# One hybrid decoder layer on one core: the last head's output rows, its decays and k's transposition in another order, and a wider pin in the first feed-forward stage

## The chip, the cores and the metric

The kernel runs on one core of one Trainium2 chip. The metric is the time of one execution on the device in microseconds; lower is better. All arithmetic that counts is done by TensorE (PE) in pairs of a high and a low part, three products for one product of float32, so that PE is busy nearly all the time, and VectorE (DVE) and ScalarE (ACT) make the high and low parts, copy results out of PSUM and compute the nonlinear steps. GpSimd (POOL) does little, and SyncE (SP) issues nearly all transfers.

## The reference, cut to what matters

```python
x = x + 0.5 * swiglu(rms_norm(x, n1), w_gate1, w_up1, w_down1)     # FFN 1: silu(h Wg) * (h Wu), then Wd
h = rms_norm(x, mix_norm)                                          # 1024 tokens, width 1024
proj = h @ w_in                      # q, k, v, z of 8 heads of 128; z, x, B, C of 16 SSM heads; gates
qkv = silu(causal_dwconv(proj_qkv, conv_w))                        # 4 taps
q, k = l2_normalize(q) * 128**-0.5, l2_normalize(k)
decay = exp(where(incl, gc[t] - gc[s], -inf))                      # gc: running sum of log decays in a chunk of 64
a_low = where(strict, beta * (k k^T) * decay, 0); t_inv = inverse(eye + a_low)
u, w = t_inv @ (v * beta), t_inv @ (k * beta * exp(gc))
o_gdn = scan over chunks(q k^T * decay, u, w, ...)                 # state 128 x 128 per head
o_gdn = rms_norm(o_gdn, w_n) * silu(z)
o_ssm = rms_norm(ssd(...) * silu(z_ssm), ...)                      # Mamba-2, in two groups of 512
x = x + concat(o_gdn, o_ssm) @ w_out                               # 2048 rows of w_out
x = x + 0.5 * swiglu(rms_norm(x, n2), w_gate2, w_up2, w_down2)     # FFN 2
out = rms_norm(x, final_norm)
```

## The kernel before

The program is written once, in the order of its stages, and a scheduler puts the instructions of each engine in a row: it takes them by the order of the program where operands are ready by its own reckoning, and by explicit pins (`tc.issue_after(e)`: what is written inside is placed behind instruction `e`). On the chip each engine then works its row off from the front.

**FFN.** Each of the two feed-forward stages forms gate and up products by seven products of half-size blocks in place of eight (`a_ops` and `b_ops` make sums of blocks on DVE, `split` makes the high part on ACT, line 241, and the low part on DVE, line 242). `gate_up_all` goes over 22 tiles of weights (`for i, (p, w) in enumerate(todo)`), gate and up in turn; PE's products are lines 334 to 336, copies out of PSUM line 343, the gate's silu line 380 or 462. In the first stage a side stream is mixed into this loop: `win_units` reads columns of `w_in` (`wraw`), forms the seven combinations of four of the heads' weights, splits them (`wunit`, ACT 241 and DVE 242) and stores them in DRAM (`wu_scr`), and each `next(side)` issues one such piece. The loop issues none for tiles under 4, and for tile 4 a first one in the first half (only loads) and two in the second half. Line 433 decides which halves of tile 4 pin these pieces behind the sums and splits (`made`) of the same half.

**Mixer.** Four units of the SSM come first, then 8 heads (`for h in range(GH)`). Heads 0 to 3 (`h < NESTED`) project q and k (`conv_silu`: product, four taps, silu), then v and z (`proj_half`), with the weights split on the spot (lines 123 to 125 on PE). Heads 4 to 7 use the stored units (`chunk`, `unit_prod`, lines 1259 to 1261 on PE). For each head `decays` (not yet a function before) loads the running sums into `dt`, exponentiates them to `qe` (line 1361) and, block by block, to `dt` (line 1364, eight small ACT instructions, behind POOL's causal mask). `k_part` transposes k on PE (line 1345, two PSUM banks called `ps_mx`) and reads each of the 8 blocks twice on ACT: `jd` (line 1349, the squared norm) and `kd` (line 1350, k scaled by a decay). Then follow the products of k with k and q (lines 1426 and 1427, again `ps_mx` banks), small inverse steps (products of 32 and 64 columns, lines 1496 to 1522, and many small DVE instructions `fx`, `ft`), and the recurrence.

**Output projection.** The output rows are summed in `xa`. `group_tile(n, b, dh, w, m)` multiplies one group of 256 rows of `w_out` (`w`, high and low part) with the normalised SSM outputs (`m`, called `mtt`): six products into one `ps_pj` bank (lines 123 to 125, operands `w` and `mtt`), and ACT copies the bank to `xa` with a scale (line 1220) for group 0. `out_start` loads rows and outputs of group 0 on POOL's queue, splits the rows (`w0`, ACT 241, DVE 242) and makes `mtt` (`ssm_split`: high on ACT, line 1200, low on DVE, line 1201); `group_prep(1)` does the same for group 1. The first 8 tiles (`FIRST_TILES = 4` blocks by two halves) are drawn into the last head, h = 7, ahead of its k products, which are pinned behind the last of those tiles (`tile_end`).

## Time and profile before

| what | value |
|---|---|
| median of 3 runs | 2318.16 us (2317.92 to 2319.36) |
| the profiled execution | 2318.03 us, span 2316.3 us |
| PE busy | 2267.1 us, 98% of the span |
| DVE, ACT, POOL busy | 76%, 51%, 2% |
| mean granted clock of PE | 0.993 |

The span reaches from the first to the last recorded instruction; 1.7 us of the profiled execution lie outside it. PE's granted clock is 1.00 nearly everywhere and 0.50 in a few stretches. A row of the timeline has the start, the duration, the engine, the line, the operation, what it writes and reads, and in brackets how long the engine had stood idle and which instruction ended the wait. The durations of PE's rows overlap; the spacing of their starts is what one costs.

### The profile page before, as it was taken

The numbers are of one execution on the slowest core, as the hardware profiler recorded it, in microseconds if no ns is written. First come the engines' busy times: TensorE is split into PE (matmuls) and PEld (weight loads), VectorE is DVE, ScalarE is ACT, GpSimd is POOL, SyncE is SP. The second block draws the span as 40 slices with busy tenths as digits, with TensorE's granted clock in tenths as the row PEclk, the third lists the DMA queues.
The fourth block names the chain that finished last, engine by engine and source line by source line (L and its number), as shares of the span: only waits on it lengthen the run. The fifth ranks groups of instructions, "written<-read, shape, count | busy, mean of one in ns | idle before, by whom it ended". The sixth has DMA issues, their size and how long they took to land.

```text
span 2316.3 us, 31987 instructions
## 1 busy us (share of the span) xinstructions
PE 2267.1 (98%) x11654; PEld 1848.9 (80%) x11654; DVE 1753.3 (76%) x3217; ACT 1179.7 (51%) x2284; POOL 50.6 (2%) x117
## 2 busy tenths in 40 slices
PE   7999999999999999999999998999999999999998
PEld 5788888888878878877877776888878888888886
DVE  8998987769777787656667778578698777766787
ACT  7444433354367985874655557432443333334344
POOL 0000000000000110000000000000000000000000
PEclk9999999999999999999999999899999999999999
DMA  3467663496653343242356556335223333329445
GB/s 111 159 210 241 228 207 115 170 334 214 210 187 125 128 128 98 69 128 65 83 165 180 168 172 216 103 98 191 91 72 119 109 106 109 104 89 357 138 154 214
DMA packets 262194, 356.96 MB, mean 154 GB/s; under 512 B 60808, under 2 KB 167404, under 8 KB 260244
## 3 DMA queue, kind: packets, MB, share of 16 engines
q1 hardware_dynamic: 261364, 352.73, 46.7%
q8 instruction: 91, 1.49, 0.3%
q0 software_dynamic: 672, 2.19, 0.2%
q14 instruction: 67, 0.55, 0.1%
HBM read 249.34 MB, written 105.52 MB: 153 GB/s over the span
## 4 chain that ended last, share of the span: by engine, by line
PE 79%; DVE 9%; ACT 7%; DMA 2%; issue 2%; POOL 0%; SPq 0%; DVEq 0%; ACTq 0%; POOLq 0%
PE ps_pj L124 6%; PE ps_pj L123 6%; PE ps_pj L125 6%; PE ps_pj L334 6%; PE ps_pj L335 6%; PE ps_pj L336 6%; PE ps_mx L334 3%; PE ps_mx L336 3%; PE ps_mx L335 3%; PE ps_pj L564 2%; PE ps_pj L565 2%; PE ps_pj L563 2%; PE ps_pj L1259 2%; PE ps_pj L1261 2%; PE ps_pj L1260 2%
## 5 line engine op out<-in xcount | busy, mean ns | idle before, releaser
L336 PE MATMUL ps_pj<-bh,al 128*128 128x512 f32 x688 | 267.9, 389 | 0.0
L335 PE MATMUL ps_pj<-bl,ah 128*128 128x512 f32 x688 | 267.8, 389 | 0.0
L334 PE MATMUL ps_pj<-bh,ah 128*128 128x512 f32 x688 | 267.5, 390 | 0.0
L125 PE MATMUL ps_pj<-hhi,wlo 128*128 128x512 f32 x576 | 229.9, 399 | 0.0
L123 PE MATMUL ps_pj<-hhi,whi 128*128 128x512 f32 x576 | 229.4, 398 | 0.4 <-ACT gsb L901 0.4
L124 PE MATMUL ps_pj<-hlo,whi 128*128 128x512 f32 x576 | 228.9, 397 | 0.0
L335 PEld LDWEIGHTS ps_pj<-bl,ah 128*128 128x128 f32 x688 | 129.2, 188 | 26.7
L336 PEld LDWEIGHTS ps_pj<-bh,al 128*128 128x128 f32 x688 | 129.2, 188 | 26.7
L334 PEld LDWEIGHTS ps_pj<-bh,ah 128*128 128x128 f32 x688 | 129.0, 188 | 26.6
L242 DVE TENSOR_TENSOR al<-as,ah 128x512 fp32r<-128x512 f32 x220 | 141.1, 685 | 7.3 <-ACT ah L241 6.8
L317 DVE TENSOR_TENSOR as<-wst 128x512 f32<-128x512 f32 x220 | 144.3, 684 | 2.5 <-DMA wst<-in_ffn_w_up_dram 2.4
L241 ACT CAST ah<-wst 128x512 fp32r<-128x512 f32 x88 | 54.5, 621 | 179.1 <-PE ps_oo L335 116.7
L241 ACT CAST hid<-hraw 128x1024 fp32r<-128x1024 f32 (+1 forms) x84 | 82.2, 980 | 123.6 <-PE ps_oo L565 45.6
L334 PE MATMUL ps_mx<-bh,ah 128*128 128x512 f32 x352 | 139.3, 398 | 5.2 <-ACT sg L380 2.1
L335 PE MATMUL ps_mx<-bl,ah 128*128 128x512 f32 x352 | 139.0, 395 | 0.4 <-DVE bl L242 0.4
L336 PE MATMUL ps_mx<-bh,al 128*128 128x512 f32 x352 | 138.2, 393 | 1.0 <-DVE al L242 1.0
L241 ACT CAST ah<-as 128x512 fp32r<-128x512 f32 x220 | 125.2, 617 | 19.6 <-DVE as L317 19.5
L123 PEld LDWEIGHTS ps_pj<-hhi,whi 128*128 128x128 f32 x576 | 108.4, 188 | 21.6 <-ACT gsb L901 0.9
L124 PEld LDWEIGHTS ps_pj<-hlo,whi 128*128 128x128 f32 x576 | 108.4, 188 | 21.4 <-issue 0.8
L125 PEld LDWEIGHTS ps_pj<-hhi,wlo 128*128 128x128 f32 x576 | 108.3, 188 | 20.9 <-issue 0.5
L242 DVE TENSOR_TENSOR hid<-hraw,hid 128x1024 fp32r<-128x1024 f32 (+1 forms) x84 | 95.0, 1131 | 26.6 <-ACT hid L241 26.3
L343 ACT COPY m<-ps_pj 128x512 f32<-128x512 f32 x88 | 51.6, 588 | 112.9 <-PE ps_pj L336 112.7
(502 smaller groups left out, 5651.6 us busy)
## 6 DMA issues: line engine op xcount, KB each, us to landing
hraw<-hid_scr SPq DMA_DIRECT2D x70, 512.0 KB, 4.3
wu_scr<-wunit SPq DMA_DIRECT2D x112, 256.0 KB, 3.2
wunits<-wu_scr SPq DMA_DIRECT2D x56, 512.0 KB, 4.7
hid_scr<-hs SPq DMA_DIRECT2D x110, 256.0 KB, 3.0
wst<-in_ffn_w_down_dram SPq DMA_DIRECT2D x50, 512.0 KB, 4.7
wst<-in_ffn_w_gate_dram SPq DMA_DIRECT2D x22, 1024.0 KB, 5.6
wst<-in_ffn_w_up_dram SPq DMA_DIRECT2D x22, 1024.0 KB, 5.5
hid_scr<-sg SPq DMA_DIRECT2D x44, 256.0 KB, 2.0
```

The lines of the kernel that those rows point to most:

```text
L123: T.matmul(o, lhsT=wh, rhs=mh, start=first, stop=False)
L124: T.matmul(o, lhsT=wh, rhs=ml, start=False, stop=False)
L125: return T.matmul(o, lhsT=wl, rhs=mh, start=False, stop=last)
L241: return (A.copy(out=hi, in_=src), V.tensor_tensor(out=lo, in0=src, in1=hi.bitcast(F32), op=ALU.subtract))
L242: V.tensor_tensor(out=lo, in0=src, in1=hi.bitcast(F32), op=ALU.subtract))
L317: V.tensor_tensor(out=t, in0=v[0], in1=v[1], op=v[2])
L334: T.matmul(bank, lhsT=wh[:, k], rhs=bh[:, k], start=a, stop=False, skip_group_check=True)
L335: T.matmul(bank, lhsT=wh[:, k], rhs=bl[:, k], start=False, stop=False, skip_group_check=True)
L336: T.matmul(bank, lhsT=wl[:, k], rhs=bh[:, k], start=False, stop=z, skip_group_check=True)
L343: A.copy(out=t, in_=bank)
L563: T.matmul(bank, lhsT=hh, rhs=wh, start=first and k == 0, stop=False, skip_group_check=True)
L564: T.matmul(bank, lhsT=hh, rhs=wl, start=False, stop=False, skip_group_check=True)
```

## The change

Three things change. First, line 433 drops its second condition, so that the two pieces of the side stream in the second half of tile 4 are pinned too. Second, for heads 0 to 3 `k_part` stands behind the projections of v and z and the store of z, not ahead of them. Third, for head 7 the tiles of group 0 come ahead of `k_part`, of the decays (now a function) and of v's taps; `mtt` of group 0 is made ahead of the split of `w0`; `kd` is made on DVE; `z_scr` is stored by POOL's queue; and `group_prep(1)` comes behind the k products in the program and is pinned behind the sixth copy to `xa` (`moved[5]`).

```diff
@@ gate_up_all, prep
-                        if i == 4 and grp == 0:
+                        if i == 4:
                             for e in made:
                                 pins.enter_context(tc.issue_after(e.ins))
@@ group_tile
-            A.mul(out=o, in_=p, mul=r)
+            moved.append(A.mul(out=o, in_=p, mul=r))
@@ out_start
         for j in range(2):
+            ssm_split(0, j, y, *m)
+        for j in range(2):
             split(w[0][:, j], w[1][:, j], x[:, j])
-            ssm_split(0, j, y, *m)
@@ k_part
-                    A.mul(out=kd[:, b], in_=pt[:, i * P:(i + 1) * P], mul=wend[:, b, h:h + 1])
+                    if h == GH - 1:
+                        V.tensor_scalar(out=kd[:, b], in0=pt[:, i * P:(i + 1) * P],
+                                        scalar1=wend[:, b, h:h + 1], scalar2=None, op0=ALU.mult)
+                    else:
+                        A.mul(out=kd[:, b], in_=pt[:, i * P:(i + 1) * P], mul=wend[:, b, h:h + 1])
@@ for h in range(GH)
+            if h < GH - 1:
+                qe, dt = decays(h)
...
                 conv_silu(g1, wa, 1, cw_g, 8 + h, kt)
-                tk, br2, kd = k_part(h, kt)
                 wa = next_w()
...
-                tk, br2, kd = k_part(h, kt)
+                if h < GH - 1:
+                    tk, br2, kd = k_part(h, kt)
                 with tc.issue_after(copy.ins):
                     A.activation(out=qt, in_=qt, func=AF.Silu)
-                if h == GH - 1:
+                if h < GH - 1:
+                    conv_from(pre, 16 + h, vt_)
+                    A.activation(out=zc, in_=zc, func=AF.Silu)
+                    A.activation(out=vt_, in_=vt_, func=AF.Silu)
+                else:
                     out_start()
-                conv_from(pre, 16 + h, vt_)
-                A.activation(out=zc, in_=zc, func=AF.Silu)
-                A.activation(out=vt_, in_=vt_, func=AF.Silu)
-            nc.sync.dma_start(out=z_scr[h], in_=zc)
-            if h == GH - 1:
-                ready1 = group_prep(1)
-                for b in range(FIRST_TILES):
-                    for dh in range(2):
-                        tile_end = group_tile(0, b, dh, *ready0[0])
+                    for b in range(FIRST_TILES):
+                        for dh in range(2):
+                            tile_end = group_tile(0, b, dh, *ready0[0])
+                    tk, br2, kd = k_part(h, kt)
+                    qe, dt = decays(h)
+                    conv_from(pre, 16 + h, vt_)
+                    A.activation(out=zc, in_=zc, func=AF.Silu)
+                    A.activation(out=vt_, in_=vt_, func=AF.Silu)
+            (G if h == GH - 1 else nc.sync).dma_start(out=z_scr[h], in_=zc)
+            if h < NESTED:
+                tk, br2, kd = k_part(h, kt)
...
+            if h == GH - 1:
+                with tc.issue_after(moved[5].ins):
+                    ready1 = group_prep(1)
```

ACT's row in the first feed-forward stage, where tile 4's first sums are split and the gate's silu (`sg`, line 380) frees the PSUM banks of the tile before; ahead of the change:

```order
L241 CAST bh_651<-bs 128x512 x2
L241 CAST ah<-wst 128x512
L241 CAST wunit<-wraw 128x512
L241 CAST ah<-as 128x512
L380 ACT_TABLE_LOAD
L380 ACTIVATE sg_759<-ps_pj 128x512
L380 ACTIVATE sg_760<-ps_mx 128x512
```

and now:

```order
L241 CAST bh_651<-bs 128x512 x2
L241 CAST ah<-wst 128x512
L241 CAST ah<-as 128x512
L380 ACT_TABLE_LOAD
L380 ACTIVATE sg_759<-ps_pj 128x512
L380 ACTIVATE sg_760<-ps_mx 128x512
```

The cast of the first weight piece has left this place; it now stands 48 instructions further back in ACT's row.

ACT's row in head 0, from the decays on; before, with the blocks of transposed k on both sides of the eight `dt`:

```order
L1361 ACT_TABLE_LOAD
L1361 ACTIVATE qe<-dt 128x1024
L1349 ACTIVATE jd,tk<-ps_mx 128x128
L1350 ACTIVATE kd<-ps_mx,wend 128x128
L1349 ACTIVATE jd,tk<-ps_mx 128x128
L1350 ACTIVATE kd<-ps_mx,wend 128x128
L1349 ACTIVATE jd,tk<-ps_mx 128x128
L1364 ACTIVATE dt<-dt,ngc 128x128 x8
L1350 ACTIVATE kd<-ps_mx,wend 128x128
```

and now (`pre` and `zc` are v's and z's projections):

```order
L1392 COPY pre<-ps_pj 128x512
L1393 ACT_TABLE_LOAD
L1393 ACTIVATE zc<-ps_pj 128x512
L1369 ACT_TABLE_LOAD
L1369 ACTIVATE dt<-dt,ngc 128x128 x8
L1392 COPY pre<-ps_pj 128x512
L1366 ACTIVATE qe<-dt 128x1024
L1293 ACTIVATE vt__8416<-pre,cols 128x1024
L138 CAST whi<-wst 128x8x128
L1393 ACT_TABLE_LOAD
L1393 ACTIVATE zc<-ps_pj 128x512
L1350 ACTIVATE jd,tk<-ps_mx 128x128
```

The blocks of k have moved behind the eight `dt` and behind v and z; on PE 47 products stand between the old and the new place of the eight transposes.

ACT's row in head 7; before, from the end of `k_part` to the first copies to `xa` (`vt_`, v's first tap; `whi`, the rows of group 1):

```order
L1350 ACTIVATE kd<-ps_mx,wend 128x128
L1200 ACTIVATE mtt<-y_13586,cols 128x1024
L1292 ACTIVATE vt__13327<-pre,cols 128x1024
L1406 ACT_TABLE_LOAD
L1406 ACTIVATE zc<-zc 128x1024
L138 CAST whi<-wst 128x1024 x2
L1407 ACTIVATE vt__13327<-vt__13327 128x1024
L1200 ACTIVATE mtt<-nat,cols 128x1024 x2
L1220 ACTIVATE xa<-ps_pj,rg_7158 128x512 x3
```

and now, from the operands of group 0 to the same copies:

```order
L1200 ACTIVATE mtt<-y_13531,cols 128x1024 x2
L241 CAST w_13534<-x_13530 128x1024 x2
L1366 ACT_TABLE_LOAD
L1366 ACTIVATE qe<-dt 128x1024
L1293 ACTIVATE vt__13312<-pre,cols 128x1024
L1369 ACTIVATE dt<-dt,ngc 128x128 x2
L1220 ACTIVATE xa<-ps_pj,rg_7158 128x512
L1369 ACTIVATE dt<-dt,ngc 128x128
L1220 ACTIVATE xa<-ps_pj,rg_7158 128x512
L1369 ACTIVATE dt<-dt,ngc 128x128 x3
L1220 ACTIVATE xa<-ps_pj,rg_7158 128x512
```

Both `mtt` stand together, ahead of the decays, and the copies to `xa` begin between the eight `dt`. Further on (not shown) the blocks `jd`, the rows and outputs of group 1 and `qsq` (the square of q) stand between the eighth and the ninth copy to `xa`.

## The prediction

> **What bounds the kernel.** I read the page's first part, then what PE waits for, then PE's granted clock by stretches, and then ACT's timeline at the three places that the change touches. The page says that PE is the bound, and that its granted clock (tenths, 40 slices) falls in few places:

> ```profile
> PE 2267.1 (98%) x11654; PEld 1848.9 (80%) x11654; DVE 1753.3 (76%) x3217; ACT 1179.7 (51%) x2284; POOL 50.6 (2%) x117
> ...
> PEclk9999999999999999999999999899999999999999
> ```

> So a change that leaves PE's products as they are can win only PE's waits, and time in which PE runs at a lower clock. The waits, grouped by what ended them (us in total, times, longest):

> ```profile
> PE ps_pj L123 <- ACT xa L1220: 4.9, 2, 4.7
> ...
> PE ps_pj L123 <- ACT mtt L1200: 2.9, 1, 2.9
> PE ps_mx L1426 <- ACT kd L1350: 2.5, 3, 1.4
> PE ps_mx L334 <- ACT sg L380: 2.1, 1, 2.1
> PE ps_mx L1345 <- ACT kt L862: 1.8, 2, 1.6
> ...
> PE ps_mx L334 <- ACT m L343: 1.4, 2, 0.7
> ...
> PE ps_mx L336 <- DVE al L242: 1.0, 1, 1.0
> ```

> Five of them lie where the change works: `sg` in the first feed-forward stage, `kd` and `kt` in the plain heads, `mtt` and `xa` in head 7. The clock is the fourth figure from the right here (after PE, PEld, DVE, ACT and POOL busy; then DMA share and GB/s):

> ```profile
> 74.05:77.46 3.41, 3.41 (x8) 2.73 (x9) 2.93 (x5) 2.05 (x4) 0.00 (x0) 0.50 0.00 0
> ...
> 1005.00:1011.00 6.00, 4.46 (x26) 3.82 (x27) 2.97 (x17) 5.95 (x21) 0.00 (x0) 1.00 0.01 1
> ...
> 1428.44:1435.97 7.53, 3.58 (x15) 2.07 (x13) 5.87 (x19) 7.51 (x31) 0.30 (x1) 1.00 0.64 180
> 1435.97:1439.38 3.41, 2.93 (x6) 1.82 (x6) 3.41 (x6) 3.40 (x4) 0.00 (x0) 0.50 0.31 48
> ...
> 1442.80:1459.86 17.06, 15.99 (x133) 11.79 (x134) 6.76 (x11) 9.35 (x15) 0.00 (x0) 0.50 0.39 128
> 1428.44:1460.13 31.69, 22.76 (x157) 15.92 (x155) 19.46 (x37) 23.46 (x51) 0.30 (x1) 0.68 0.46 137
> ```

> Behind the waits of 2.1, 2.9 and 4.7 us the clock is 0.50, in steps of 3.41 us; around the waits of 1.4 us and under (the second row) it stays 1.00. What one 128x512 product costs at each clock:

> ```profile
> 70.62 0.39 PE L335 MATMUL ps_pj<-bl,ah 128*128 128x512 f32 x1
> ...
> 71.52 0.39 PE L336 MATMUL ps_pj<-bh,al 128*128 128x512 f32 x1
> 74.05 0.79 PE L334 MATMUL ps_mx<-bh,ah 128*128 128x512 f32 x1 [2.13 <-ACT sg L380]
> ...
> 76.77 0.63 PE L334 MATMUL ps_mx<-bh,ah 128*128 128x512 f32 x1
> ```

> Four spacings in 0.90 us are 0.225 us each at full clock; six in 2.72 us are 0.45 us at half. A microsecond at 0.50 thus loses half a microsecond.

> **The pin (A).** PE waits at 74.05 because ACT held the queue:

> ```profile
> 70.45 0.62 ACT L241 CAST wunit<-wraw 128x512 fp32r<-128x512 f32 x1 [3.44 <-DMA wraw<-in_w_in_dram]
> 70.98 0.62 ACT L241 CAST ah<-as 128x512 fp32r<-128x512 f32 x1
> 71.61 1.28 ACT L380 ACT_TABLE_LOAD   x1
> 72.91 0.60 ACT L380 ACTIVATE sg<-ps_pj 128x512 f32<-128x512 f32 x1
> 73.40 0.59 ACT L380 ACTIVATE sg<-ps_mx 128x512 f32<-128x512 f32 x1
> ```

> The weight piece waits 3.44 us for its transfer, and `ah`, the table load and both `sg` stand behind it. Without it, ACT goes on as soon as `as` and PE's bank are there; PE ends its bank at about 71.9 (71.52 plus 0.39), one `sg` takes 0.5 us, so the second `sg` ends near 72.6 and PE waits about 0.75 instead of 2.13: 1.4 won. A wait of that length left the clock alone elsewhere, so the 3.41 us at half rate go too: 1.7. The wait of 1.0 for `al` (DVE, which is then no longer given two pieces to subtract) should shrink by 0.3 or so; `m` L343 (0.7 here, the same in the second feed-forward stage, which has no side stream: 2 times) stays. Sum 3.4. The pieces cost the same later, 48 instructions on in ACT's row, where five of them now come close together; at 0.6 us each (the first row), on DVE as on ACT, up to 3 us could show as a PE wait if no slack is there. The stores `wu_scr` move with them and stand in SP's queue ahead of one tile's weight load; PE waits for no such load in the list above, and I count nothing. Bounds: 0.4 (all but 3 us of it eaten) to 4.5.

> **Plain heads (B).** Head 0 and head 3 show the loss:

> ```profile
> 1002.38 2.45 ACT L1364 ACTIVATE dt<-dt,ngc 128x128 f32<-128x128 f32 x8 [0.96 <-POOL dt L970]
> ...
> 1005.64 0.49 PE L1426 MATMUL ps_mx<-kt 128*128 128x128 f32 x2 [1.42 <-ACT kd L1350]
> ...
> 1007.70 0.49 PE L1426 MATMUL ps_mx<-kt 128*128 128x128 f32 x2 [0.90 <-ACT kd L1350]
> ...
> 1181.11 1.09 PE L1345 MATMUL ps_mx<-ident,kt 128*128 128x128 f32 x8 [1.62 <-ACT kt L862]
> ```

> ```profile
> 1178.70 1.28 ACT L862 ACT_TABLE_LOAD   x1 [6.38 <-DVE kt L847]
> ```

> Before, ACT waits for POOL's mask with `kd` behind it, and the k products wait for the banks; in head 3 the transposes wait for the silu of k. Together 3.9 us. With the transposes 47 products (10.6 us) later in head 0, k's silu is long done. But the k products now follow only 18, 16, 12 and about 10 products behind the transposes, and ACT needs 0.5 us for each `jd` and `kd` (rows below), so 2.0 for the first bank and 4.0 for both. In head 0, 18 products (4.1 us) cover the first bank; `whi` of head 1 and the later banks I count with 1.7 together. In heads 1 and 2, 3.6 and 2.7 us cover it; in head 3 about 2.3 do, and I count 0.6. So 2.3 of new waits against 3.9: 1.6 won. Bounds: 3.9 (all covered) and, with 1.2 us of wait in each of four heads (the mean of head 0's two) ahead of these 2.3, a loss of 3.2.

> **Head 7 (C).** From the windows, the stretch takes 31.69 us; at full clock its work is 3.58 + 2.93/2 + 15.99/2 + 0.27 = 13.3 us, so 18.4 are lost: 8.9 in waits, the rest at half clock. The rows that hold it up on ACT:

> ```profile
> 1420.38 2.44 ACT L1567 ACTIVATE vr<-vr,co 128x128 f32<-128x128 f32 x8
> ...
> 1425.09 1.98 ACT L241 CAST w<-x 128x1024 fp32r<-128x1024 f32 x2
> ...
> 1429.33 0.25 ACT L1349 ACTIVATE jd<-ps_mx 128x128 bf16<-128x128 f32 x1
> ...
> 1433.32 1.23 ACT L1200 ACTIVATE mtt<-y,cols 128x1024 fp32r<-128x1024 f32 x1
> ...
> 1435.61 1.28 ACT L1406 ACT_TABLE_LOAD   x1
> ...
> 1437.87 1.98 ACT L138 CAST whi<-wst 128x1024 fp32r<-128x1024 f32 x2
> ...
> 1441.02 2.17 ACT L1200 ACTIVATE mtt<-nat,cols 128x1024 fp32r<-128x1024 f32 x2
> 1443.10 1.82 ACT L1220 ACTIVATE xa<-ps_pj,rg 128x512 f32<-128x512 f32 x3
> ```

> The second `mtt` is behind 16 instructions on k (4.0 us); the first copies to `xa` behind group 1's rows and outputs, and PE has no free `ps_pj` bank until then. Now `vr` starts where one `mtt` stood ahead of it (1420.38 - 1.04), and two `mtt` (as the 2.17 of group 1) and `w0` follow: 1419.34 + 2.44 + 2.1 + 2.0 = 1425.9. DVE sets the next limit:

> ```profile
> 1426.36 0.68 DVE L1269 TENSOR_TENSOR pre<-ps_pj,pre 128x512 f32<-128x512 f32 x1
> ...
> 1428.29 1.21 DVE L242 TENSOR_TENSOR w<-x,w 128x1024 fp32r<-128x1024 f32 x1
> ```

> ```profile
> 1427.65 1.03 PE L1345 MATMUL ps_mx<-ident,kt 128*128 128x128 f32 x8
> ```

> The low part of `w0` now comes straight behind the sum `pre` (first row; about 1427.0, when both `mtt` low parts are done), with small steps of head 6 between: 1428.4 and 1429.8 for its two halves. PE, free at 1427.65 (its transposes stand elsewhere now), waits 1.5 us in tile 1. The 42 other products run to 1440; the copies go between `dt`, table load and silu, and tile 7 waits perhaps 0.4 for its bank. Then comes what is late next: behind the eighth copy ACT has `jd`, `whi`, `jd`, group 1's `mtt` (2.17), `jd`, `qsq` (1.0) and `jd` before the ninth: 0.6 + 4 x 0.25 + 1.0 + 2.2 + 1.0 and the copy's 0.6, from 1440.6 to about 1447. PE has 19 products (4.3 us) until it needs that bank, near 1445: 2.0 us of wait. That lies between 1.6 (no drop of the clock) and 2.13 (drop), so I add one step at half rate, 1.7. Loss now 1.5 + 0.4 + 2.0 + 1.7 = 5.6, won 12.8. `kd` on DVE has no row; eight of 128x128 cost between nothing and the 0.68 of 128x512 each, and I take ACT's 0.25 (the `jd` row), 2.0 in all, beside PE. So runs POOL's z store, behind which only clears for later steps stand, and the load of `dt`, which moves two places back in SP's queue. Head 7's k products come some 10 us later; no wait for its recurrence stands among PE's waits, so I count nothing for that. Bounds: 6 and 17.

> Sum: 3.4 + 1.6 + 12.8 = 17.8. The profiled execution took 2318.03, 0.13 under the median of 2318.16; 2318.03 - 17.8 = 2300.2.

> [...] The windows above show 15.99 us of PE work in 17.06 us without the clock coming back, and the drop at 74.05 behind 2.13 us of idleness. [...]

> **Rivals.** *The clock stays low in head 7.* If the ninth copy's wait drops the clock just ahead of head 7's small inverse products, it may stay low as it did for 17.06 us before: five steps, of which I counted one. Four more at 1.7 are 6.8, so 2307.0. For it: that row. Against: the wait is shorter than 4.65, and fewer gaps surround it.

> *No drop and the covers hold.* If ACT comes to the ninth copy within 1.6 us the clock never drops: C 15.5, B 2.5, A 4.4, 2295.6. For it: the page's row of the clock shows its one low slice from 1447.7 (25 slices of 57.9) on, so heads 4 to 6, with the same small products, ran without such a drop. [...]

> *The pin wins nothing.* If five pieces on a full DVE give back 3 us, 2303.2.

> *Slower.* The k products wait for ACT in all four plain heads. The price per head would be head 0's 2.3 again, a table load of 1.28 and one step of half clock, 1.7: 5.3, and 21 for four. It decides from there: A and C bring 16.2, so each head must lose 5.2 before the kernel is slower by 0.2%. Against it: ACT stood idle 6.38 us before head 3's silu (row above), and 10 to 18 products stand between.

> **Chances.** Forecast 0.48 (its own range 2297 to 2304), clock low 0.24, covers hold 0.13, pin nothing 0.08, a gain of under 4.6 us 0.04, slower 0.03. 0.2% is 4.6 us, about what a measurement here can tell from no change, so the first four are all faster: 0.93; same 0.04, slower 0.03. The range reaches from 2294 (the covers hold and a little more) to 2309 (the clock low and the pin half lost).

> **What would show it.** In the changed profile: no wait for `sg` L380 over 1 us and clock 1.00 from 74 to 78 (A); no waits for `kd` or `kt` over 1 us near 1005 and 1181, and how long the k products (now L1443) wait for banks (B); the wait for `w` L242 in tile 1 near 1.5 us, the wait for `xa` L1220 at about 2 us in place of 4.7, and 0.50 for one step at most between 1420 and 1450 (C). The forecast fails if ACT's order in head 7 is worked off later than I count, since everything there hangs on the ninth copy, or if the k products wait in heads that had no wait before.

## The result and the profile after

| | before | after |
|---|---|---|
| median | 2318.04 us (2313.91 to 2319.36, 4 runs) | 2296.61 us (2295.60 to 2297.22, 4 runs) |
| profiled execution, span | 2318.03, 2316.3 us | 2296.60, 2294.9 us |
| mean granted clock | 0.993 | 0.998 |

The ratio is 0.9909, 95% interval [0.9894, 0.9924]: 21.4 us faster, where the prediction said 17.8 (2300.2; range 2294 to 2309). Two runs among those behind this document, one of the kernel before and one with ten tiles, took 3794 and 3750 us at a mean clock of 0.56 and are left out of every median. Where the gain came from is read from the starts of the same product in both traces:

| product of PE | before | after | shift | won in the stage |
|---|---|---|---|---|
| first `ps_pj<-bh,ah` of FFN 1 | 37.96 | 38.49 | +0.53 | start-up, -0.53 |
| 89th `ps_mx<-bh,ah`, well behind tile 4 | 249.43 | 246.38 | -3.05 | pin (A): 3.58 |
| last `ps_mx<-sq,ones`, ahead of head 0 | 987.97 | 983.91 | -4.06 | end of FFN 1: 1.01 |
| last product of the stored units in head 7 | 1427.41 | 1419.97 | -7.44 | plain heads (B), with the later heads' projections: 3.38 |
| last product of the pair tiles | 1619.16 | 1596.26 | -22.90 | head 7 (C): 15.46 |
| 265th `ps_mx<-bh,ah`, in FFN 2 | 1889.31 | 1867.91 | -21.40 | start of FFN 2: -1.50 |

What PE waits for now, the rows that answer to those of before:

```profile
PE ps_pj L123 <- ACT xa L1220: 2.3, 2, 2.0
...
PE ps_mx L334 <- ACT m L343: 1.3, 2, 0.7
...
PE ps_mx L334 <- ACT sg L380: 0.8, 1, 0.8
...
PE ps_mx L1443 <- ACT kd L1355: 0.8, 2, 0.4
...
PE ps_mx L336 <- DVE al L242: 0.3, 1, 0.3
```

`mtt` and `kt` are gone from the list, `sg` fell from 2.1 to 0.8, `xa` from 4.9 to 2.3, `kd` from 2.5 to 0.8 (and these two waits lie in later heads, at 1304 and 1364). ACT at tile 4 of FFN 1, and PE's wait:

```profile
70.18 0.62 ACT L241 CAST ah<-as 128x512 fp32r<-128x512 f32 x1 [2.64 <-DVE as L317]
70.82 1.28 ACT L380 ACT_TABLE_LOAD   x1
72.11 0.60 ACT L380 ACTIVATE sg<-ps_pj 128x512 f32<-128x512 f32 x1
72.61 0.59 ACT L380 ACTIVATE sg<-ps_mx 128x512 f32<-128x512 f32 x1
```

```profile
73.25 0.50 PE L334 MATMUL ps_mx<-bh,ah 128*128 128x512 f32 x1 [0.84 <-ACT sg L380]
```

ACT no longer sits behind `wraw`'s transfer; it waits for DVE's sums, as it should.

In head 0 the cover of the k products was all but enough:

```profile
1007.48 0.27 ACT L1350 ACTIVATE jd<-ps_mx 128x128 bf16<-128x128 f32 x1
...
1009.23 0.42 ACT L1355 ACTIVATE kd<-ps_mx,wend 128x128 f32<-128x128 f32 x1
```

```profile
1009.70 0.49 PE L1443 MATMUL ps_mx<-kt 128*128 128x128 f32 x2
```

The fourth `kd` of the first bank ends at 1009.65 and PE's product starts at 1009.70. That is 0.39 us behind the start of the product before it, where 0.23 is usual, so the cover fell short by about 0.15 us.

In head 7, DVE's low parts of `w0`, ACT ahead of the ninth copy, and PE:

```profile
1419.36 1.22 DVE L242 TENSOR_TENSOR w<-x,w 128x1024 fp32r<-128x1024 f32 x1
...
1420.59 1.22 DVE L242 TENSOR_TENSOR w<-x,w 128x1024 fp32r<-128x1024 f32 x1
```

```profile
1434.27 1.08 ACT L138 CAST whi<-wst 128x1024 fp32r<-128x1024 f32 x1
...
1435.47 2.22 ACT L1200 ACTIVATE mtt<-nat,cols 128x1024 fp32r<-128x1024 f32 x2
...
1437.80 1.09 ACT L1468 ACTIVATE qsq<-qt 128x1024 f32<-128x1024 f32 x1
...
1438.99 0.73 ACT L1220 ACTIVATE xa<-ps_pj,rg 128x512 f32<-128x512 f32 x1
```

```profile
1439.78 0.50 PE L123 MATMUL ps_pj<-w,mtt 128*128 128x512 f32 x1 [1.96 <-ACT xa L1220]
```

The new wait is where the prediction had it, behind `whi`, `mtt` and `qsq`, and 1.96 us long. The clock, in windows cut on the grid of its changes (told below; PE busy is the first figure behind the length, the clock the third from the right, not the fourth as the prediction has it):

```profile
1420.20:1452.00 31.80, 29.51 (x237) 22.70 (x235) 23.31 (x52) 26.47 (x55) 2.69 (x3) 1.00 0.43 138
1435.81:1439.22 3.41, 2.01 (x9) 1.30 (x7) 3.41 (x5) 3.41 (x8) 0.00 (x0) 1.00 0.38 58
1439.22:1442.64 3.42, 2.87 (x45) 2.34 (x45) 1.97 (x6) 3.38 (x12) 0.00 (x0) 1.00 0.74 184
1678.16:1681.57 3.41, 1.62 (x6) 1.06 (x7) 3.34 (x6) 1.42 (x3) 0.00 (x0) 1.00 1.03 350
1681.57:1684.98 3.41, 3.41 (x10) 2.63 (x9) 3.29 (x6) 2.03 (x4) 0.00 (x0) 0.50 0.72 238
```

A stretch of 31.80 us in head 7 now has 29.51 us of PE work at full clock; before, 31.69 us had 22.76 at a mean of 0.68. And a step of half clock has appeared at 1681, at the start of FFN 2, where the code is the same and the waits are too.

### The profile page after: what moved, and what is told of

Its sections match the earlier page's. It is cut to its first block, busy times and chain, and to the rows that moved or that the text cites. A ratio compares the mean times of both kernels' runs of the same rounds, so it can differ in the third digit from the quotient of the medians.

```text
span 2294.9 us, 31984 instructions
## 1 busy us (share of the span) xinstructions
PE 2257.9 (98%) x11654; PEld 1842.1 (80%) x11654; DVE 1751.5 (76%) x3225; ACT 1178.9 (51%) x2276; POOL 52.1 (2%) x118
## 3 DMA queue, kind: packets, MB, share of 16 engines
q0 software_dynamic: 816, 2.72, 0.3%
## 4 chain that ended last, share of the span: by engine, by line
PE 87%; ACT 6%; DVE 5%; issue 1%; DMA 1%; POOL 0%; SPq 0%; DVEq 0%; POOLq 0%; ACTq 0%
PE ps_pj L125 7%; PE ps_pj L123 7%; PE ps_pj L124 7%; PE ps_pj L335 6%; PE ps_pj L334 6%; PE ps_pj L336 6%; PE ps_mx L334 3%; PE ps_mx L336 3%; PE ps_mx L335 3%; PE ps_pj L564 2%; PE ps_pj L565 2%; PE ps_pj L563 2%; PE ps_pj L1260 2%; PE ps_oo L335 2%; PE ps_pj L1261 2%; PE ps_oo L334 2%
## 5 line engine op out<-in xcount | busy, mean ns | idle before, releaser
L336 PE MATMUL ps_pj<-bh,al 128*128 128x512 f32 x688 | 268.1, 390 | 0.0
L335 PE MATMUL ps_pj<-bl,ah 128*128 128x512 f32 x688 | 267.9, 389 | 0.0
L334 PE MATMUL ps_pj<-bh,ah 128*128 128x512 f32 x688 | 267.7, 390 | 0.0
L123 PE MATMUL ps_pj<-hhi,whi 128*128 128x512 f32 x576 | 229.4, 398 | 0.4 <-ACT gsb L901 0.4
L336 PEld LDWEIGHTS ps_pj<-bh,al 128*128 128x128 f32 x688 | 129.2, 188 | 26.7
L335 PEld LDWEIGHTS ps_pj<-bl,ah 128*128 128x128 f32 x688 | 129.2, 188 | 26.6
L334 PEld LDWEIGHTS ps_pj<-bh,ah 128*128 128x128 f32 x688 | 129.0, 188 | 26.7
L241 ACT CAST hid<-hraw 128x1024 fp32r<-128x1024 f32 (+1 forms) x84 | 82.2, 980 | 123.9 <-PE ps_oo L565 46.3
L241 ACT CAST ah<-wst 128x512 fp32r<-128x512 f32 x88 | 54.5, 621 | 176.4 <-PE ps_oo L335 113.4
L242 DVE TENSOR_TENSOR al<-as,ah 128x512 fp32r<-128x512 f32 x220 | 141.1, 685 | 4.8 <-ACT ah L241 4.3
L334 PE MATMUL ps_mx<-bh,ah 128*128 128x512 f32 x352 | 138.6, 396 | 3.9 <-ACT m L343 1.3
L335 PE MATMUL ps_mx<-bl,ah 128*128 128x512 f32 x352 | 138.3, 393 | 0.5 <-DVE bl L242 0.5
L336 PE MATMUL ps_mx<-bh,al 128*128 128x512 f32 x352 | 137.8, 391 | 0.3 <-DVE al L242 0.3
L241 ACT CAST ah<-as 128x512 fp32r<-128x512 f32 x220 | 125.1, 618 | 24.1 <-DVE as L317 24.1
L123 PEld LDWEIGHTS ps_pj<-hhi,whi 128*128 128x128 f32 x576 | 108.4, 188 | 21.8 <-ACT gsb L901 0.8
L242 DVE TENSOR_TENSOR hid<-hraw,hid 128x1024 fp32r<-128x1024 f32 (+1 forms) x84 | 95.0, 1131 | 26.3 <-ACT hid L241 26.1
L343 ACT COPY m<-ps_pj 128x512 f32<-128x512 f32 x88 | 51.4, 587 | 111.7 <-PE ps_pj L336 111.4
```

The source lines that it names most:

```text
L123: T.matmul(o, lhsT=wh, rhs=mh, start=first, stop=False)
L241: return (A.copy(out=hi, in_=src), V.tensor_tensor(out=lo, in0=src, in1=hi.bitcast(F32), op=ALU.subtract))
L242: V.tensor_tensor(out=lo, in0=src, in1=hi.bitcast(F32), op=ALU.subtract))
L334: T.matmul(bank, lhsT=wh[:, k], rhs=bh[:, k], start=a, stop=False, skip_group_check=True)
L335: T.matmul(bank, lhsT=wh[:, k], rhs=bl[:, k], start=False, stop=False, skip_group_check=True)
L336: T.matmul(bank, lhsT=wl[:, k], rhs=bh[:, k], start=False, stop=z, skip_group_check=True)
```

## The experiments

My theory behind the result: each part wins the waits that its trace names, the parts add up, and in head 7 the gain comes from taking `k_part`, the decays and group 1's operands out of ACT's way. Against it stood that the parts depend on each other, that single edits inside the head matter or do nothing, and that the clock, not the order, made part of the difference. All ratios are to the kernel before, run beside.

### The three parts alone

The pin alone is the first hunk of the diff (the condition stands on line 436, not on line 433 as the description of the kernel has it), the plain heads alone the two hunks that move `k_part` for `h < NESTED`, the last head alone all the rest.

> The kernel before with the wider pin alone. Theory: the pin is worth 3.6 us by itself (the wait for sg falls from 2.13 to about 0.8 us and the 3.41 us of half clock behind it go; the later bunch of weight pieces costs nothing): about 2314.5 us. Rival: part of those 3.6 us came with the other two parts or from a luckier execution, and the bunch of pieces takes back what the wait gives: 2317 or more, with new waits for al or ah between 110 and 150 us.

> The kernel before with the later k_part in heads 0 to 3 alone. Theory: no new waits for the k products, 3.4 us won: about 2314.7 us, no wait for kd or kt over 0.5 us between 990 and 1250 us. Rival (the prediction's count): new waits of 2.3 us in these heads, 1.6 us won, 2316.5 us; what the changed kernel shows there then depends on its other parts.

> The kernel before with the last head's part alone. Theory: 15.5 us won by itself, about 2302.6 us; the wait for the ninth copy to xa is about 2.0 us as in the changed kernel and the clock stays at 1.00 through the stretch. Rival: the wait at that place is close to the length that lowers the clock, and with another phase it does: one step of 3.41 us at 0.50 or five of them, so 2304.3 to 2311 us.

| kernel | median us | ratio, 95% interval |
|---|---|---|
| pin alone | 2315.26 (10 runs, 2310.97 to 2318.09) | 0.9987 [0.9978, 0.9996] |
| plain heads alone | 2314.43 (10 runs) | 0.9983 [0.9973, 0.9992] |
| last head alone | 2301.40 (4 runs) | 0.9929 [0.9914, 0.9944] |

The product of the three is 0.9899, inside the interval of the whole, so within that noise (some 5 us either way) the parts add up.

The pin's median is 2.65 us below the kernel before, with runs 7 us apart; in its profile the stage of the 89th product is 3.59 us shorter (the whole change: 3.58). The two differ for a reason. Of the five profiles without the pin, two (the plain heads alone, the last head alone) have the wait for `sg` but no step of half clock behind it, and there the same stage is about 1.5 us shorter than in the kernel before. So the pin wins 3.6 us where that step would have fallen and about 2.1 us where not; the median lies between.

The plain heads' median is 3.48 us below the kernel before, but their profile puts only 1.72 us of it between the product ahead of head 0 and the end of the stored units. Another 2.59 us were won ahead of head 0, where this edit changes nothing. No wait for `kd` or `kt` over 0.3 us is left in heads 0 to 3. Over all nine profiles with this edit the stretch is 1.7 to 3.4 us shorter than before, 2.7 on average; the whole change, with 3.38, is the highest.

The profile of the plain heads alone also holds a control for the clock. The wait for `sg` is there, 2.0 us, and this time costs no step (the third window is taken up in the last section):

```profile
PE ps_mx L334 <- ACT sg L380: 2.0, 1, 2.0
```

```profile
69.70:73.11 3.41, 1.91 (x9) 1.26 (x7) 2.15 (x4) 3.03 (x5) 0.00 (x0) 1.00 0.51 154
73.11:76.53 3.42, 2.88 (x12) 2.36 (x13) 2.40 (x4) 2.06 (x5) 0.00 (x0) 1.00 0.00 0
1424.79:1428.20 3.41, 1.66 (x7) 0.99 (x6) 1.06 (x7) 3.41 (x20) 0.30 (x1) 1.00 0.84 301
```

The wait is cut by a line of the clock's grid into 1.5 and 0.5 us. The last head alone has no wait for the ninth copy at all; its 1.4 us are waited by the k products for `kd` on DVE, since the scheduler put other tiles there, and the clock holds:

```profile
PE ps_mx L1442 <- DVE kd L1352: 1.4, 1, 1.4
```

Its head 0 shows the reverse of the control. The two waits of 1.4 and 0.9 us that cost no step in the kernel before now fall into one window:

```profile
1002.36:1005.77 3.41, 1.56 (x10) 0.97 (x8) 0.00 (x0) 3.41 (x19) 0.00 (x0) 1.00 0.01 2
1005.77:1009.18 3.41, 2.87 (x10) 2.59 (x11) 2.78 (x16) 3.36 (x8) 0.00 (x0) 0.50 0.00 0
```

### What carries the gain in head 7

Group 1's preparation alone, in the kernel before:

```diff
-                ready1 = group_prep(1)
                 for b in range(FIRST_TILES):
...
+            if h == GH - 1:
+                with tc.issue_after(moved[5].ins):
+                    ready1 = group_prep(1)
             fs_u = dram.tile([4, NB, 32, 32], F32, name="fs_u", bufs=2)
```

> The kernel before with one edit in the last head: group 1's preparation (whi and mtt from nat on ACT) behind the k products and pinned behind the sixth copy to xa; k_part, the decays and v's taps stay ahead of the tiles. Theory: this alone takes the 4.65 us wait for the first copies and the half clock behind it (17.07 us, 8.5 lost); the waits for the second mtt (2.9 and 0.7 us) and one step of half clock stay: 10 to 12.5 us won, 2305.5 to 2308 us. Rival: the gain of 15.5 hangs on the tiles standing ahead of k_part, and this alone gives under 5: 2313 us or more.

2305.73 us, ratio 0.9946 [0.9930, 0.9962]: 12.0 us under the median of the kernel before beside it (2317.70), and 12.7 us in the stage of head 7 by the trace, from this one edit, as the theory had it. The waits for `xa` are gone, those for `mtt` stay:

```profile
PE ps_pj L123 <- ACT mtt L1200: 2.9, 1, 2.9
```

and the small inverse products, the same as in the 17.07 us at half clock before, run at full clock:

```profile
1440.21:1457.28 17.07, 17.06 (x186) 13.87 (x185) 9.83 (x19) 13.37 (x20) 0.00 (x0) 1.00 0.27 97
```

The other way round, the last head's part alone with group 1's preparation ahead of the tiles:

```diff
                     out_start()
+                    ready1 = group_prep(1)
                     for b in range(FIRST_TILES):
...
-            if h == GH - 1:
-                with tc.issue_after(moved[5].ins):
-                    ready1 = group_prep(1)
```

> The last head's part alone, but with group 1's preparation ahead of the tiles in the program as it was before. Theory: ACT now has 2.0 us of whi and 2.2 of mtt between the operands of group 0 and the copies; the first copies come late by up to 2 us and a wait of 1 to 3 us for them appears in the tiles, with a step of half clock at times: 2303 to 2307 us against 2301.4. Rival: with k_part and dt out of the way ACT has room for both, and the later copies gain what the first lose: 2300 to 2302 us.

2300.90 us, ratio 0.9928 [0.9912, 0.9944], against 2301.40 with the preparation late: the theory fell, the rival held. In its profile the list of PE's waits is empty between 1410 and 1470. So the late preparation is worth 12.7 us in the order of before, and nothing that shows once the rest of the last head's part is in. By the traces head 7 even won more with the early preparation, 17.9 us against 16.5. Either edit takes the 4.65 us wait; only the reordering also takes the wait for the second `mtt`. Which piece of the reordering does that is argued from ACT's row and not shown: the tiles ahead of `k_part`, `mtt` ahead of the split of `w0` and the store of z were not run singly, nor was the whole change with the early preparation.

`kd` back on ACT, in the changed kernel:

```diff
-                    if h == GH - 1:
+                    if False:
                         V.tensor_scalar(out=kd[:, b], in0=pt[:, i * P:(i + 1) * P],
```

> The changed kernel with kd of head 7 back on ACT. Theory: the eight kd (about 0.25 us of ACT's queue each) stand with the eight jd ahead of group 1's operands and the ninth copy, so the wait there grows by about 2 us to 4 us, and the clock drops for at least one step: 2300 to 2306 us. Rival: ACT has slack there, since DVE's share of the banks was the later one; the time stays within 1 us of 2296.6.

2295.76 us (2294.43 to 2301.15), ratio 0.9903 [0.9884, 0.9921]: the theory fell, the rival held. PE's waits in the stretch sum to 2.4 us as against 2.3, but for another reason:

```profile
PE ps_mx L1443 <- DVE dt L1450: 1.6, 1, 1.6
```

The scheduler moved k products ahead of the twelfth tile (the one that waits for the ninth copy), so they meet the late engine first; the tile itself then waits 0.47 us. Moving `kd` to DVE brought nothing that can be measured.

The decays back ahead of the projections:

```diff
-            if h < GH - 1:
-                qe, dt = decays(h)
+            qe, dt = decays(h)
...
-                    qe, dt = decays(h)
                     conv_from(pre, 16 + h, vt_)
```

> The changed kernel with the last head's decays (a table load, qe and eight dt, 4.8 us of ACT) back ahead of the projections in the program, so that on ACT dt stands ahead of the split of w0. Theory: the first tile waits for w0 by some 2.5 us more, of which about 1 comes back because the copies are no longer broken up by dt and the ninth copy is earlier: 2298 to 2300 us, with one step of half clock if the wait exceeds 1.8 us within one window. Rival: the tiles' start is set by DVE (the low part of w0 behind v's sums) and not by ACT, so nothing changes or the earlier ninth copy even wins: 2294.6 to 2296.6 us.

2297.25 us (2295.43 to 2301.41), ratio 0.9906 [0.9891, 0.9921]. It lies between the two: the first tiles wait 0.6 and 0.9 us for `w0`, with one step of half clock in the profiled execution, and the wait for the ninth copy is gone. By the median the decays' place is worth nothing that can be measured.

### The wait for the ninth copy, and the clock

One more square of q on ACT ahead of the ninth copy, then the square on DVE instead:

```diff
-            A.activation(out=qsq, in_=qt, func=AF.Square)
+            for _ in range(2 if h == GH - 1 else 1):
+                A.activation(out=qsq, in_=qt, func=AF.Square)
```

> The changed kernel with the square of q computed twice in head 7, which puts about one more microsecond on ACT ahead of the ninth copy to xa, so that PE's wait there grows from 1.96 to about 2.9 us. Theory (in all profiles so far the clock changes stand on one grid of 3.413 us, and it falls where PE is idle for about 1.8 us or more within one such window): 2.9 us of waiting fall into one window by more than 1.8 unless they are split evenly, so the clock drops to 0.50 there in about four of five executions, for one to five steps of 3.41 us: 2296.6 + 0.9 + 1.7 to 8.5, so 2299 to 2306 us. [...]

2301.43 us, ratio 0.9922 [0.9903, 0.9941], the four runs at 2297.33, 2300.13, 2302.74 and 2306.39 us with mean clocks of 0.999, 0.998, 0.997 and 0.995. The wait came to 2.0 us, not 2.9, and stood at the k products (`kd` on DVE), because the tiles were reordered again; but all of it fell into one window, and the next ran at half clock:

```profile
1437.77:1441.19 3.42, 1.40 (x7) 0.83 (x6) 3.24 (x6) 3.42 (x9) 0.00 (x0) 1.00 0.42 65
1441.19:1444.60 3.41, 3.41 (x23) 2.66 (x25) 1.05 (x3) 3.36 (x12) 0.00 (x0) 0.50 0.90 307
```

So 2.02 us of idleness in one window at full clock (3.42 less 1.40) were followed by half clock, as the theory has it. The result, within the theory's 2299 to 2306, also fits steps that fall differently from run to run: the mean clocks differ by 0.004, which over 2300 us is 9.2 us, as much as the times do.

```diff
-            A.activation(out=qsq, in_=qt, func=AF.Square)
+            if h == GH - 1:
+                V.tensor_tensor(out=qsq, in0=qt, in1=qt, op=ALU.mult)
+            else:
+                A.activation(out=qsq, in_=qt, func=AF.Square)
```

> The changed kernel with the square of q of head 7 made on DVE, which stands idle there. Theory: the ninth copy to xa comes about 1 us earlier on ACT (and group 1's second mtt no longer between four k blocks), the wait of 1.96 us falls to about 0.9 or less, and no window is idle enough to lower the clock: about 2295.5 us. Rival: the wait moves to the k products (ps_mx banks read by kd on DVE) and nothing is won: 2296.6 us or more.

2298.51 us, ratio 0.9910 [0.9895, 0.9924]: nothing won, the theory fell, and the rival's place is wrong too, since the wait for the ninth copy is still 2.02 us. The microsecond went from ACT to DVE, and ACT now waits for DVE between the k blocks:

```profile
1439.44 0.28 ACT L1350 ACTIVATE jd<-ps_mx 128x128 bf16<-128x128 f32 x1 [1.41 <-DVE kd L1352]
```

### More tiles ahead of k_part

```diff
-    FIRST_TILES = 4
+    FIRST_TILES = 6
...
-                with tc.issue_after(moved[5].ins):
+                with tc.issue_after(moved[9].ins):
```

> The changed kernel with twelve tiles ahead of the last head's k_part in place of eight (FIRST_TILES 6) and group 1's preparation pinned behind the tenth copy. Theory: the 1.96 us wait for the ninth copy comes from group 1's mtt, whi and qsq ahead of it on ACT; with these behind the copies it falls under 0.5 us and the kernel gains 1.5 to 2 us on the changed one, about 2294.9 us. Rival: the wait only moves on, to the k products of head 7 or to the tiles of group 1, and the time is that of the changed kernel within 0.5 us or worse.

2304.57 us, ratio 0.9947 [0.9930, 0.9964]. The wait for the ninth copy went, as expected, and the rival held (the wait moves on), at another place and with a larger price:

```profile
PE ps_pj L123 <- DVE xt L1632: 7.2, 1, 7.2
```

Head 7's last scaling (`vr`) starts at 1574.7 us, against 1557.4 in the changed kernel; DVE's last products for the pair tiles stand behind it, and PE runs dry at 1579. The prediction had counted nothing for a later chain of head 7; it has slack, but less than 17 us. With ten tiles (FIRST_TILES 5, `moved[7]`):

> The changed kernel with ten tiles ahead of the last head's k_part (FIRST_TILES 5) and group 1's preparation pinned behind the eighth copy. Theory: the ninth and tenth copy stand ahead of group 1's mtt, PE's wait there falls from 1.96 to under 1 us, and head 7's chain, some 3 us later, still ends ahead of the rows that need it (with twelve tiles it ended 17 us later and PE waited 7.2 us): about 2295 us. Rival: the chain ends more than 10 us later again and PE waits for the pair tiles: 2299 us or more.

2299.27 us (three runs, 2296.64 to 2299.93), ratio 0.9915 [0.9898, 0.9933]; PE waits 0.6 us for a copy to `xa`, two tiles further on, and 1.1 us for `xt`:

```profile
PE ps_pj L123 <- DVE xt L1632: 1.1, 1, 1.1
```

The profiled execution also carried a wait of 2.4 us at the end of FFN 1 with a step of half clock, which the edit doesn't touch, so whether ten tiles win or lose is not settled by it. With `kd` on ACT as well:

> As the run with ten tiles, but with kd of head 7 back on ACT, so that the k blocks no longer pass from ACT to DVE and back one by one. Theory: the eight blocks are done in one go of 4 us, the k products get their banks no later than with kd on DVE, and the time is that of ten tiles or 0.5 to 1 us better: 2294 to 2295 us. Rival: the 4 us hold up the eleventh copy and group 1's mtt, and a wait of 2 us with a step of half clock comes back: 2298 us.

2295.03 us (2294.13 to 2295.61), ratio 0.9900 [0.9882, 0.9918]. Between 1410 and 1470 PE is busy for 59.26 us, against 57.71 in the changed kernel:

```profile
1410.00:1470.00 60.00, 59.26 (x394) 46.86 (x393) 42.84 (x112) 49.24 (x111) 3.27 (x8) 1.00 0.63 203
```

It is the fastest version tried. Its median is 1.6 us under the changed kernel's 2296.61 and the ranges only touch (2295.61 and 2295.60), but the two were not run beside each other and their intervals overlap, so that it beats it is likely and not shown.

## Why the prediction was right

**The pin.** Its term was 3.4; 3.58 was measured in the traces, 2.65 by the medians of the pin alone. 1.7 of the term is the step behind `sg`, which the kernel before does not pay in every execution. The wait for `sg` came out at 0.84 us (predicted 0.75), the half clock from 74 to 77 went, the wait for `al` fell to 0.3. No wait came from the bunched weight pieces or the held load.

**Plain heads.** The mechanism was right, the size off: 1.6 predicted, 3.38 measured in this pair of traces and 2.7 on average over the nine profiles with the edit. The step that failed is "2.3 of new waits": none over 0.15 us came in heads 0 to 3, and 0.4 twice in later heads. In head 0 the count "18 products (4.1 us) cover the first bank" missed by about 0.15 us; what I added on top for `whi` and the later banks was covered.

**Head 7.** 12.8 predicted, 15.46 measured. "2.0 us of wait" for the ninth copy was 1.96, found by adding up ACT's row; the wait of tile 7 was 0.30 (0.4). Two terms were too dear. "Waits 1.5 us in tile 1" came to about 0.45 us spread over the first two tiles (12 products in 3.16 us, where 2.7 would do): DVE's low parts ended 0.4 and 0.5 us sooner behind PE's first product than I had them (0.38 and 1.61 us in place of 0.75 and 2.15), and the scheduler had put tile 2's products with the high parts between tile 1's, and I had counted the first tile alone. And "one step at half rate, 1.7" did not come, though not for the reason that I weighed (a length between 1.6 and 2.13): the 1.96 us were cut by a grid line into 1.40 and 0.56. In the run with two squares, where 2.02 us of idleness fell into one window, the step came; in another execution the 1.96 us could have cost it too, so that saving is luck. The result, 2296.61, lies 0.4 us below the forecast's own range (2297 to 2304) and nearest to the rival "no drop and the covers hold" (2295.6). The rival's numbers for the total and for C came out, its condition (ACT at the ninth copy within 1.6 us) did not.

**Not foreseen.** 1.01 us at the end of FFN 1, where a wait for `xtb` was 0.94 us before, under 0.15 after, 1.7 with only the last head's preparation changed and 2.4 with ten tiles; nothing in the change explains that spread, so I take it as the execution's, which is not shown. And the step at the start of FFN 2, 1.50 us lost: the two waits there are 1.35 and 0.55 us in both profiles, but in the kernel before a grid line cut the first. That loss is luck as well, the other way.

## What to carry to other kernels

Where one engine is the bound, write down what stands in each other engine's row ahead of the instruction that frees its buffers, and add it up: here that gave the new wait to 0.04 us. Look for waits of about 2 us as costs that come and go: by the position of the clock's grid the wait for `sg` cost a step of 3.41 us at half clock in the kernel before (2.13 us, whole in one window) and none in the plain heads alone (2.0 us, cut into 1.5 and 0.5). A wait is removed by taking either of the two things ahead of it away; test them singly, since the second may bring nothing, as the late preparation and `kd` on DVE did here. And a moved chain has slack only up to a point: twelve tiles ahead of it in place of eight cost 8 us at a place some 140 us later.

## What the runs showed of the hardware

```profile
70.64:74.05 3.41, 1.28 (x7) 0.74 (x5) 1.47 (x3) 3.38 (x6) 0.00 (x0) 1.00 0.27 94
```

```profile
1423.39:1426.81 3.42, 1.70 (x6) 0.80 (x6) 3.38 (x7) 3.40 (x6) 0.30 (x1) 1.00 0.88 307
1426.81:1430.22 3.41, 3.41 (x10) 2.67 (x9) 3.37 (x4) 2.04 (x3) 0.56 (x1) 0.50 0.32 62
```

So in these runs about half a window of idleness, one wait or several together, cost a step of 3.41 us at half rate (up to 1.7 us lost), even where PE had worked for 1.70 us of the window. Whether a wait of about 2 us did so depended on where the grid fell in that execution: 2.13 us whole in one window did, 1.96 and 2.0 us cut in two did not. That this may hold for waits up to 3.5 us, twice the 1.76 us that cost no step, is an estimate.

What stays open is the rule for the way back. Most drops ended after one window (3.41 us, as at 74.05 and 1435.97 before and at 1681.57 after), but the one at 1442.80 before lasted five, with 15.99 us of PE work in it, and the pin alone and the plain heads alone show the same five (a mean clock of 0.83 from 1410 to 1470 in all three). The small products by themselves did not lower the clock in the run with the late preparation (17.07 us with them at 1.00, above). The windows at half clock show a pattern: I counted 18 in which products with a weight tile of 128x128 (the `128*128` in PE's rows) filled 2.88 us or more, all followed by full clock, and 13 in which they filled 2.48 us or less, none followed by it. In the kernel before they filled 3.41 and 2.93 us of the two single steps, and 1.34, 2.48, 1.59, 1.61 and 3.39 us of the five windows, where products with tiles of 32x32 and 64x64 took most of the rest of PE's time; in the changed kernel they filled all 3.41 us of its one step. Whether the tile's size is the cause was not tried.
